# A streaming encoder step on one core: the Silu of c taken once, the cached keys and values split later, a weight split moved behind an eviction

## The chip, the core and the metric

The kernel runs on one core of one Trainium2 chip. Five engines work side by side, each with its own instruction stream: PE (matrix products), ACT (activations and copies), DVE and POOL (elementwise work) and SP (here it only issues DMA transfers). They wait for one another through semaphores. The metric is the device time of one execution in microseconds (us).

## The reference

One trunk layer of a streaming encoder for 1024 prompt tokens and 32 sample tokens, model width 1024, all in float32:

```
mod = silu(c) @ w_ada + b_ada          # six vectors: sh1, sc1, gt1, sh2, sc2, gt2
h   = rmsnorm(x, g_mix) * (1 + sc1) + sh1
u   = h @ w_in                         # attention q, k, v; mLSTM q, k, v, gates; merge gates
ya  = band attention (8 heads x 64, 64-frame chunks, 8 chunks back, relative bias);
      the sample tokens attend to 128 cached keys and values and to themselves
ym  = mLSTM matrix memory (4 heads x 128), head rmsnorm, sigmoid output gate
x   = x + gt1 * ((sigmoid(ga) * (ya @ w_br_att) + sigmoid(gm) * (ym @ w_br_mlstm)) @ w_out)
x   = x + gt2 * ((silu(g) * up) @ w_down),   g, up = split((rmsnorm(x, g_ffn) * (1 + sc2) + sh2) @ w_gate_up)
y   = rmsnorm(x, g_final)
```

There are two vectors c, one for the prompt and one for the sample, of 1024 numbers each. Outputs are y, the new keys and values and the new mLSTM states.

## The kernel before

**Numbers in two parts.** A float32 operand is split into a high part, a copy in the PE's own rounded float32 format, and a low part, the difference. A product is three passes (high by high, low by high, high by low). So each operand costs one copy, mostly on ACT, and one subtraction, on DVE or POOL (`split_to`, L364 and L365; for tokens in head layout `split_heads`, L662 to L665).

**Tokens and blocks.** The 1056 tokens are columns, in three tiles of 352. The input projection runs in blocks of 128 output columns. `unit` (L395) makes one block and one tile: 24 matmuls into one PSUM bank of the pool `mm` (three banks). Each block then has a `put` that evicts the bank.

**Weights.** `Weights.advance` (L67) keeps a queue of blocks: it splits the next blocks while at most two are ahead of the one in use (L364 on ACT, L365 on POOL), and issues the load of a later block on SP (L375), which waits until the raw tile that it overwrites has been split.

**The order of the work is written out by hand** for PE, ACT, DVE and POOL: the order of the program is the order on each engine. Work beside the blocks is placed by `Side`. `unit` calls `side.flush(1)` behind k = 2, 4 and 6, which runs one entry of the list `side.later`, and `side.tick()` behind k = 1, 3, 5 and 7, which advances the generators that run beside the blocks: the attention of a pair of heads (22 steps over a segment) and `ada_rest`.

**The beginning.** `first_units` (L429) computes the first two of the six modulation vectors from `csil`, the Silu of c in column layout (`silu_cols`, L281, from the tile `cols` loaded at L213), on PE (`ada_sums`, L318); `ada_done` (L325) evicts them on ACT (L326, L327). Then come the norm and the first three blocks: keys, values and queries of the first pair of heads. The first two tiles are done for all three blocks at once; the third tile of keys and values is accumulated in the two banks of `psS`. The last line of `first_units`, L565, calls `W.advance()`, which splits the key weights of the second pair of heads. Only then `k_block(0)` (run, L608) evicts the third tile of its keys (`put`, L595 to L606: ACT L601 and L604, DVE L606) and calls `W.advance()` itself (L612). `v_block(0)` (L644) evicts the third tile of its values (L642) and appends four entries to `side.later` (L653): the two halves of the values to be transposed (`v_tail`, L667: PE L674, ACT L662, DVE L665, and with the second half the output copy L631 and its DMA), the sample's values (`v_sample`, L679), and `cache_kv`. `q_block(0)` computes its third tile with `unit`; its `put` is L702, L704, L706 and L686.

**The cached keys and values** are loaded early (L735 to L739). `cache_kv` (L741) splits the keys (ACT L748 twice, DVE L750 twice, each over 64 partitions x 512) and the values (DVE L664 and L665). They are needed by the ninth query tile of each head.

**Attention** (L763). Step i transposes the probabilities of item i - 2 (PE L819 into `psT`, ACT L826, DVE L831), makes the scores of item i (PE L792 into `psS`, DVE L806 adds the bias and takes the maximum, ACT L807 the exponent, DVE L811 and POOL L812 the normalisation) and applies item i - 3 to the values (PE L851 into `psV`, then ACT L857, DVE L858 and L859). `psS`, `psT` and `psV` exist once each.

**The other four modulation vectors** come from `ada_rest` (L1258), on DVE: 128 dot products (L1275) of a weight tile with a broadcast row of Silu(c). For each half of the rows it loads c into all partitions (`crow`, L1266), yields three times, takes the Silu of 128 x 1024 on ACT (L1269), and yields once more. `tmpt` tiles, among them `crow`, share four buffers.

Of the kernel before, what the change touches and what calls it, by code (L numbers as in the profile page):

```python
# [8 lines left out]
F32 = mybir.dt.float32  # L9
F32R = mybir.dt.float32r  # L10
BF16 = mybir.dt.bfloat16
AF = mybir.ActivationFunctionType
# [6 lines left out]
D = 1024  # L19
S = 1024  # L20
TS = 32
# [5 lines left out]
DH = 64  # L27
# [112 lines left out]
def hybrid_stream_step(  # L140
# [10 lines left out]
    pe, act, dve, pool, sp = nc.tensor, nc.scalar, nc.vector, nc.gpsimd, nc.sync  # L151
# [10 lines left out]
    dr = ctx.enter_context(tc.tile_pool(name="scratch", bufs=1, space=DRAM))  # L162
# [16 lines left out]
    def tmpt(shape=(P, T), dt=F32):  # L179
        return tmp.tile(list(shape), dt, tag="t", name=nm("t"))  # L180
# [16 lines left out]
    side = Side()  # L197
    W = Weights()
# [12 lines left out]
    NR = R_C + 16  # L211
    cols = cp.tile([P, NR], F32, name="cols")
    act.dma_start(cols, params)  # L213
    csil = cp.tile([P, KD, 2], F32, name="csil")

    def bc2(ap):
# [64 lines left out]
    def silu_cols():  # L281
        act.activation(csil, cols[:, R_C:R_C + 16].rearrange("p (c k) -> p k c", c=2), AF.Silu)
        dve.scalar_tensor_tensor(gb1, cols[:, R_ADA + 8:R_ADA + 16], 1.0, gm1, op0=ALU.add, op1=ALU.mult)
# [145 lines left out]
    def first_units(put_k, put_v, put_q):  # L429

        early, late = TILES[:2], TILES[2]
        act.activation(silu1, ones, AF.Silu)
        silu_cols()
        for j in range(6):
            pt = mmt()
            ada_sums(j, 0, pt)
            ada_sums(j, 1, pt)
            if j < 3:
                ada_done(j, pt)
            else:  # L440
                n = {3: 2, 4: 6, 5: KD}[j]
                for i in range({3: 0, 4: 2, 5: 6}[j], n):
                    square_sum(i, 0, CUT)
                ada_done(j, pt)
# [117 lines left out]
        for w, n in zip(W.blocks, (3, 3, 2)):  # L562
            for _ in range(n):
                W.used(w)
        W.advance()  # L565

    def units(w):
        done = first.get(id(w))
# [65 lines left out]
    def v_block(hp):  # L634
        w = w_cols(VA + hp * P)

        vfs = []

        def put(lo, hi, pt):
            if lo == 0:  # L640
                vfs.append(tmpt())
            act.activation(vfs[0][:, lo:hi], pt, AF.Copy)  # L642

        def run():  # L644
            for lo, hi, pt in units(w):
                put(lo, hi, pt)
            vf = vfs[0]
            W.advance()
            jobs = [lambda: v_tail(hp, vf, 0), lambda: v_tail(hp, vf, 1), lambda: v_sample(hp, vf)]
            if hp:  # L650
                side.later += [jobs[0], lambda: None, jobs[1], lambda: None, jobs[2]]
            else:
                side.later += jobs + [lambda: cache_kv(early_loads[0])]  # L653
        run.w = w
        run.put = put
        return run

    def split_heads(dst, src, eng=None):

        hi, lo = (dst[:, :, :, 0], dst[:, :, :, 1]) if len(dst.shape) == 5 else (dst[:, :, 0], dst[:, :, 1])  # L660
        if eng is None:
            act.activation(hi, src, AF.Copy)  # L662
        else:
            eng.tensor_copy(hi, src)  # L664
        dve.tensor_tensor(lo, src, f(hi), op=ALU.subtract)  # L665
# [64 lines left out]
    ckv_t = []  # L730
# [7 lines left out]
        sp.dma_start(ckv[:, 1], cache_v[0, 0].rearrange("t h d -> t (h d)"))  # L738
        return ckv  # L739

    def cache_kv(ckv):  # L741
        t = slot([P, 2, 2, 512], F32R)
        cv = t[:, 0].rearrange("p s c -> p (s c)").rearrange("p (h s d) -> p h s d", s=2, d=DH)
        ck = t[:, 1].rearrange("p s (g t) -> p s g t", g=4)
        k4 = ckv[:, 0].rearrange("p (g t) -> p g t", g=4)

        for hh, (u, v) in enumerate(ROWS):
            act.activation(ck[u, hh], k4[u], AF.Copy)  # L748
        for hh, (u, v) in enumerate(ROWS):
            dve.tensor_tensor(ck[v, hh], k4[u], f(ck[u, hh]), op=ALU.subtract)  # L750
        split_heads(cv, ckv[:, 1].rearrange("p (h d) -> p h d", d=DH), dve)
        ckv_t.extend([ck, cv])

    def rel_bias_tile(h):
        bt = ap_.tile([P, WIN], F32, tag="bias", name=nm("bias"))
# [7 lines left out]
    def attention(hp):  # L763
# [69 lines left out]
        def values(it, pv, w):  # L833

            hh, qi = it
            vt, vst, cv = att_v[hp], vst_t[hp], ckv_t[1]
            hd = slice(hh * DH, (hh + 1) * DH)
            if qi % 2 == 0:
                yps[0] = ps_v()
            yp = yps[0]  # L840
            if qi < 8:
                i, c, a = 2, P, (qi - 1) * P
                kb0 = max(0, qi * P - 512) // P
                yo = yp[:, (qi % 2) * 256:(qi % 2 + 1) * 256]
                terms = [(vt[:, kb0 + b, hh], pv[:, :, b * P:(b + 1) * P]) for b in range(w // P)]
            else:
                i, c, a = 1, TS, S
                yo = yp[:, :2 * TS]
                terms = [(cv[:, 2 * hp + hh], pv[:, :, :TS]), (vst[:, hh], pv[:TS, :, TS:2 * TS])]
            for b, (v, p) in enumerate(terms):  # L850
                pe.matmul(yo.rearrange("p (s c) -> p s c", s=2), v.rearrange("p s d -> p (s d)"), p,  # L851
                          start=(b == 0), stop=(b == len(terms) - 1))
            if qi % 2 == 1 or qi == 8:

                q4 = yp[:, :i * 2 * c].rearrange("p (i s c) -> p i s c", i=i, s=2)
                y = yaT[hd, a:a + i * c].rearrange("p (i c) -> p i c", i=i)
                act.activation(y, q4[DH:, :, 0], AF.Copy)  # L857
                dve.tensor_tensor(y, q4[:DH, :, 0], y, op=ALU.add)  # L858
                dve.tensor_tensor(y, q4[:DH, :, 1], y, op=ALU.add)  # L859
# [398 lines left out]
    def ada_rest():  # L1258


        junk = gp.tile([P, 512], BF16, tag="junk", name="junk", bufs=1)
        sums = gp.tile([P, 2, 4, 2, KD], F32, tag="sums", name="sums", bufs=1)
        for half in range(2):
            crow = tmpt((P, 2, 512))
            c0 = c_rows[:, half * 512:(half + 1) * 512]
            sp.dma_start(crow, bass.AP(c0.tensor, c0.offset, [[0, P], [D, 2], [1, 512]]))  # L1266
            for _ in range(3):
                yield
            act.activation(crow, crow, AF.Silu)  # L1269
            yield  # L1270
            for b in range(32):
                wa = ada_tiles.pop(half * 32 + b)
                for c in range(2):
                    at = sums[:, half, b // KD, c, b % KD:b % KD + 1]
                    dve.tensor_tensor_reduce(junk, wa, crow[:, c], 1.0, 0.0, ALU.mult, ALU.add, at)  # L1275
                    if c == 0:
                        ada_load(half * 32 + b + 1)
                    yield
        dve.tensor_tensor(amod2, sums[:, 0], sums[:, 1], op=ALU.add)
        r0 = R_ADA + 2 * KD  # L1280
        bias = cols[:, r0:r0 + 4 * KD].rearrange("p (v j) -> p v j", v=4)
        for c in range(2):
            dve.tensor_tensor(amod2[:, :, c], amod2[:, :, c], bias, op=ALU.add)
        dve.tensor_scalar(s2, s2, 1.0, None, op0=ALU.add)
        dve.tensor_tensor(s2, s2, bc2(cols[:, R_GFFN:R_GFFN + KD]), op=ALU.mult)
# [1048 lines left out]
```

## Time and profile before

| | us |
|---|---|
| runs of the kernel | 1596.14, 1597.57, 1598.13 (median 1597.57) |
| the profiled execution | 1598.06 |
| its span, first to last instruction | 1596.3 |

| engine | busy us | share of the span |
|---|---|---|
| ACT | 796.2 | 50% |
| DVE | 1105.4 | 69% |
| POOL | 421.4 | 26% |

The mean granted PE clock over the span was 0.997. In the views that follow, a row of the timeline has start, duration, engine, line, operation, output and input with partitions x elements, a count, and in brackets the idle time ahead of it with what ended it; instructions of one line are merged. A row of the windows has the stretch, its length, the busy time of PE, PEld (weight load), DVE, ACT and POOL with the number of instructions, the granted clock, the DMA share and the rate.

### The profile page before, as it was taken

The page shows a single profiled execution, that of the slowest core. Times are in us where ns is not written, and L with a number is a line of the kernel's source. Part 1 is how long each engine was busy: PE and PEld are TensorE (multiplying, and loading weights), DVE is VectorE, ACT ScalarE, POOL GpSimd, SP SyncE. Part 2 cuts the span into 40 slices and gives each one's busy share as a digit, 9 for nine tenths or more (in the row PEclk, how much of TensorE's full clock was granted, in tenths as well). Part 3 has the DMA queues.
Part 4 walks back from the last instruction along what each step waited for, and adds up shares of the span by engine and source line. Part 5 has one row for each costly group of instructions (what it writes and reads, how often), then busy time and mean ns, then how long its engine had stood idle before and what let it go on. Part 6 is the DMA issues. An engine that isn't in the chain of part 4 may idle for free.

```text
span 1596.3 us, 27296 instructions
## 1 busy us (share of the span) xinstructions
PE 1568.8 (98%) x10197; PEld 1551.1 (97%) x10197; DVE 1105.4 (69%) x2276; ACT 796.2 (50%) x1748; POOL 421.4 (26%) x439
## 2 busy tenths in 40 slices
PE   8999999999999999999999999999999999999997
PEld 8989999999999999999999999999999999999997
DVE  3756555556776835546654699998898886799755
ACT  3765463544555545444433655554544544545443
POOL 0433242433222311000012100566565650000000
PEclk9999999999999999999999999999999999999999
DMA  9213223243132322675453311213222227427444
GB/s 373 93 59 95 96 83 109 87 132 99 55 95 66 88 85 74 134 256 177 128 149 112 107 55 51 97 55 106 81 80 94 68 77 251 143 80 240 139 135 156
DMA packets 176329, 186.02 MB, mean 117 GB/s; under 512 B 11746, under 2 KB 141446, under 8 KB 176198
## 3 DMA queue, kind: packets, MB, share of 16 engines
q1 hardware_dynamic: 173542, 182.45, 36.5%
q10 hardware_dynamic: 2656, 1.83, 0.4%
q8 instruction: 80, 1.31, 0.4%
q14 instruction: 51, 0.42, 0.1%
HBM read 150.10 MB, written 34.16 MB: 115 GB/s over the span
## 4 chain that ended last, share of the span: by engine, by line
PE 88%; ACT 3%; DVE 3%; DMA 3%; issue 2%; POOL 0%; SPq 0%; ACTq 0%; DVEq 0%; POOLq 0%
PE mm L402 38%; PE psb L1869 18%; PE mm L1869 11%; PE psb L2251 3%; PE mm L946 3%; PE mm L2251 2%; PE psV L851 2%; PE psb L2115 2%; PE psS L792 1%; PE psT L819 1%; PE mm L2115 1%; DMA s<-in_w_ada_dram 1%; DMA s<-in_x_dram 1%; PE psV L1180 1%; PE psT L1182 1%
## 5 line engine op out<-in xcount | busy, mean ns | idle before, releaser
L402 PE MATMUL mm<-s,wsp 128*128 128x352 f32 x4104 | 688.6, 324 | 0.1
L402 PEld LDWEIGHTS mm<-s,wsp 128*128 128x128 f32 x4104 | 658.7, 189 | 2.2 <-issue 0.4
L365 DVE TENSOR_TENSOR wsp<-wraw,wsp 128x512 fp32r<-128x512 f32 (+1 forms) x280 | 236.8, 863 | 118.5 <-ACT wsp L364 115.7
L1869 PE MATMUL psb<-s,wsp 128*128 128x352 f32 x1611 | 271.7, 322 | 1.5 <-DVE wsp L365 0.8
L364 ACT ACTIVATE wsp<-wraw 128x512 fp32r<-128x512 f32 x336 | 200.0, 618 | 139.0 <-PE psb L1869 41.5
L1869 PEld LDWEIGHTS psb<-s,wsp 128*128 128x128 f32 x1611 | 260.6, 188 | 2.1 <-DVE wsp L365 1.1
L1869 PE MATMUL mm<-s,wsp 128*128 128x352 f32 x933 | 159.2, 322 | 0.0
L1869 PEld LDWEIGHTS mm<-s,wsp 128*128 128x128 f32 x933 | 151.2, 188 | 0.5 <-DVE wsp L365 0.3
L812 POOL TENSOR_SCALAR st<-st,mx 128x640 f32<-128x640 f32 (+5 forms) x72 | 53.5, 742 | 188.4 <-DVE mx L811 169.3
L1275 DVE CUSTOM_DVE_ANT_0 junk<-wa,t 128x512 bf16<-128x512 f32 x128 | 94.9, 742 | 1.9 <-DMA wa<-in_w_mod_dram 0.9
L365 POOL TENSOR_TENSOR wsp<-wraw,wsp 128x512 fp32r<-128x512 f32 x56 | 74.1, 1344 | 52.0 <-ACT wsp L364 50.5
L806 DVE CUSTOM_DVE_ANT_0 st<-psS,bias 128x640 f32<-128x640 f32 (+5 forms) x72 | 44.5, 618 | 58.7 <-PE psS L792 44.0
L807 ACT ACTIVATE st<-st,mx 128x640 f32<-128x640 f32 (+5 forms) x72 | 48.1, 668 | 63.4 <-DVE mx L806 62.3
L1816 POOL TENSOR_TENSOR t<-t,sl 128x352 f32<-128x352 f32 x19 | 18.4, 968 | 213.1 <-ACT sl L1814 213.1
L826 ACT ACTIVATE pT<-psT 128x640 fp32r<-128x640 f32 (+3 forms) x80 | 38.6, 494 | 61.6 <-PE psT L819 49.1
L2224 POOL TENSOR_TENSOR fst<-fst,mhalf 128x6 f32<-128x6 f32 x1 | 2.3, 2313 | 221.1 <-DVE fst L2223 221.1
L831 DVE TENSOR_TENSOR pT<-psT,pT 128x640 fp32r<-128x640 f32 (+3 forms) x80 | 44.0, 558 | 23.0 <-ACT pT L826 22.9
L1488 POOL TENSOR_TENSOR wraw<-wraw,raw 128x512 f32<-128x512 f32 x33 | 55.8, 1705 | 0.9
L946 PE MATMUL mm<-s,s 128*128 128x264 f32 (+3 forms) x432 | 54.5, 283 | 0.0
L2251 PE MATMUL psb<-s,wsp 128*128 128x352 f32 x330 | 54.2, 324 | 0.0
L2251 PEld LDWEIGHTS psb<-s,wsp 128*128 128x128 f32 x330 | 53.1, 188 | 0.1
L946 PEld LDWEIGHTS mm<-s,s 128*128 128x128 f32 (+1 forms) x432 | 51.9, 179 | 0.5
(375 smaller groups left out, 2472.5 us busy)
## 6 DMA issues: line engine op xcount, KB each, us to landing
wraw<-in_w_in_dram SPq DMA_DIRECT2D x37, 512.0 KB, 3.6
wraw<-in_w_gate_up_dram SPq DMA_DIRECT2D x33, 512.0 KB, 3.9
wa<-in_w_mod_dram SPq DMA_DIRECT2D x64, 256.0 KB, 2.6
wraw<-in_w_down_dram SPq DMA_DIRECT2D x32, 512.0 KB, 4.3
a_d<-t SPq DMA_DIRECT2D x22, 528.0 KB, 2.7
g_d<-t SPq DMA_DIRECT2D x16, 528.0 KB, 4.2
t<-g_d SPq DMA_DIRECT2D x16, 528.0 KB, 4.8
s<-in_w_ada_dram SPq DMA_DIRECT2D x16, 512.0 KB, 8.8
```

The lines of the kernel that those rows point to most:

```text
L364: act.activation(dst[:, 0], src, AF.Copy)
L365: eng.tensor_tensor(dst[:, 1], src, f(dst[:, 0]), op=ALU.subtract)
L402: pe.matmul(pt[:, :hi - lo], wt[(w0 + k) // 4][:, a, (w0 + k) % 4], xt[k][:, b, lo:hi], start=(k == 0 and q == 0), stop=(k == n - 1 and q ...
L806: dve.tensor_tensor_reduce(so, sv, bi, -1.0, 3.0e38, ALU.add, ALU.min, mx[:n, 1:2])
L807: act.activation(st[:n, :w], st[:n, :w], AF.Exp, bias=mx[:n, 1:2], scale=-1.0, accum_out=mx[:n, 2:3])
L812: pool.tensor_scalar(st[:n, :w], st[:n, :w], mx[:n, 3:4], 1.0, op0=ALU.mult, op1=ALU.mult)
L946: pe.matmul(pt[:n, :wd], hs[k][:, a, i * P:i * P + n], whl[b][:, k, :wd], start=(k == 0 and q == 0), stop=(k == KD - 1 and q == 2))
L1275: dve.tensor_tensor_reduce(junk, wa, crow[:, c], 1.0, 0.0, ALU.mult, ALU.add, at)
L1488: self.eng.tensor_tensor(a(dst), a(x), a(y), op=op)
L1869: pe.matmul(acc, wt[:, a, k], x[k][:, b], start=(start and not onto and k == 0 and q == 0), stop=(stop and k == 3 and q == 2), skip_group_ ...
L2115: pe.matmul(acc, wt[k // 4][:, u, k % 4], piece_of[k, i][:, v], start=(k == 0 and q == 0), stop=(k == KP - 1 and q == 2))
L2251: pe.matmul(acc, wt[(k - k0) // 4][:, u, (k - k0) % 4], piece_of[k, 2][:, v], start=(k == 0 and q == 0), stop=(k == NF - 1 and q == 2))
```

## The change

There are three parts.

1. At the beginning a tile `crows` of 2 partitions x 1024 is loaded with c on ACT's queue, behind the load of `cols`. Behind `silu_cols()` ACT takes its Silu and writes it to a DRAM tile `sil_d`. `ada_rest` loads `crow` from `sil_d` instead of from c, and its own Silu goes; the number of yields stays four.
2. The `W.advance()` at the end of `first_units` goes; the next call is the one in `k_block(0)`, behind the eviction of its third tile.
3. `cache_kv` becomes two functions. The entries of `side.later` are the first half of the values, nothing, the second half, the sample, four times nothing, the cached keys, nothing, the cached values. So the second half of the values and the sample come one entry later, the keys five entries later, and the values two behind these. `values` reads the tile of the cached values only where it is used.

```
+    crows = tmpt((2, D))
+    act.dma_start(crows, c_rows)
+    sil_d = dr.tile([2, D], F32, name="sil_d")
...
         silu_cols()
+        act.activation(crows, crows, AF.Silu)
+        act.dma_start(sil_d, crows)
...
             for _ in range(n):
                 W.used(w)
-        W.advance()
...
-                side.later += jobs + [lambda: cache_kv(early_loads[0])]
+                nothing = lambda: None
+                side.later += [jobs[0], nothing, jobs[1], jobs[2]] + [nothing] * 4
+                side.later += [lambda: cache_keys(early_loads[0]), nothing, lambda: cache_values(early_loads[0])]
...
-    def cache_kv(ckv):
+    def cache_keys(ckv):
         t = slot([P, 2, 2, 512], F32R)
...
+        ckv_t.extend([ck, cv])
...
         for hh, (u, v) in enumerate(ROWS):
             dve.tensor_tensor(ck[v, hh], k4[u], f(ck[u, hh]), op=ALU.subtract)
-        split_heads(cv, ckv[:, 1].rearrange("p (h d) -> p h d", d=DH), dve)
-        ckv_t.extend([ck, cv])
+
+    def cache_values(ckv):
+        split_heads(ckv_t[1], ckv[:, 1].rearrange("p (h d) -> p h d", d=DH), dve)
...
-            vt, vst, cv = att_v[hp], vst_t[hp], ckv_t[1]
+            vt, vst = att_v[hp], vst_t[hp]
...
-                terms = [(cv[:, 2 * hp + hh], pv[:, :, :TS]), (vst[:, hh], pv[:TS, :, TS:2 * TS])]
+                terms = [(ckv_t[1][:, 2 * hp + hh], pv[:, :, :TS]), (vst[:, hh], pv[:TS, :, TS:2 * TS])]
...
-            c0 = c_rows[:, half * 512:(half + 1) * 512]
+            c0 = sil_d[:, half * 512:(half + 1) * 512]
             sp.dma_start(crow, bass.AP(c0.tensor, c0.offset, [[0, P], [D, 2], [1, 512]]))
-            for _ in range(3):
+            for _ in range(4):
                 yield
-            act.activation(crow, crow, AF.Silu)
-            yield
```

## The prediction

> **What bounds the kernel now.** I read the busy shares and the chain on the page, then the list of PE's waits, then the timeline around each wait.
>
> ```profile
> span 1596.3 us, 27296 instructions
> PE 1568.8 (98%) x10197; PEld 1551.1 (97%) x10197; DVE 1105.4 (69%) x2276; ACT 796.2 (50%) x1748; POOL 421.4 (26%) x439
> ...
> PE 88%; ACT 3%; DVE 3%; DMA 3%; issue 2%; POOL 0%; SPq 0%; ACTq 0%; DVEq 0%; POOLq 0%
> ```
>
> PE is busy 98% and holds 88% of the chain. A change elsewhere counts only where it removes or makes idle time on PE, and such a gain moves all that follows forward. Its longest waits behind the start (total us, times, longest):
>
> ```profile
> PE psT L819 <- DVE pT L831: 2.5, 3, 2.0
> PE psV L851 <- ACT pT L826: 2.0, 2, 1.7
> PE mm L674 <- ACT t L642: 1.8, 1, 1.8
> PE psS L792 <- DVE mx L806: 1.4, 1, 1.4
> ```
>
> These hold nearly all that this change can win: 1.8 and 1.4 near 75 and 88 us, 1.7 at 104, 2.0 at 427. The 1.7 has a tail (a row of the windows; the last three numbers are granted clock, DMA share, GB/s):
>
> ```profile
> 104.70:108.10 3.40, 3.40 (x13) 3.40 (x14) 1.95 (x6) 0.92 (x2) 0.80 (x1) 0.50 0.00 0
> ```
>
> For 3.4 us behind that wait PE works at half the clock.
>
> **Part 1: Silu at the beginning.** Added on ACT: the issue of a load of 2 x 1024 floats, one Silu, the issue of a write.
>
> ```profile
> cols<-in_params_dram ACTq DMA_DIRECT2D x1, 62.0 KB, 4.2
> 5.00 0.22 ACT L282 ACTIVATE csil<-cols 128x16 f32<-128x16 f32 x1 [2.25 <-DMA cols<-in_params_dram]
> 10.97 0.36 ACT L326 ACTIVATE s<-mm,gb,cols 128x2 f32<-128x2 f32 x1 [5.75 <-PE mm L321]
> 5.27 23.53 PE L321 MATMUL mm<-csil,s 128*128 128x128 f32 x192 [5.27 <-ACT csil L282]
> 98.25 1.28 ACT L1269 ACT_TABLE_LOAD   x1
> 99.54 1.06 ACT L1269 ACTIVATE t<-t 128x1024 f32<-128x1024 f32 x1
> 101.00 1.28 ACT L807 ACT_TABLE_LOAD   x1
> 65.70 0.38 SPq L1266 DMA_DIRECT2D t<-in_c_rows_dram  x1
> ```
>
> The load's issue falls into ACT's 2.25 us wait for cols. The Silu (1.06, as L1269) and the write's issue (about 0.4) fall into its 5.75 us of idle time; the Silu table is active already. PE waits only for csil, which stands ahead. Taken: 0. Bounds: nothing below, since nothing is removed here; above, the lateness of the new load, see the slower rival. The row of c is read by SP only at 65.70, when its tile comes free, long after the write. The new tile takes one of four, but is free by some 10 us, before the third of the old ones is asked for.
>
> **Part 2: the two Silus of ada_rest go,** each with two table loads: 1.28 + 1.06 + 1.28 = 3.62 us of ACT. The yields stay four, so nothing else in that generator moves. What stood behind the first:
>
> ```profile
> 103.24 0.38 ACT L857 ACTIVATE t<-psV 64x256 f32<-64x256 f32 x1
> 99.38 0.82 DVE L806 CUSTOM_DVE_ANT_0 st<-psS,bias 128x640 f32<-128x640 f32 x1 [0.95 <-POOL st L812]
> 101.72 0.63 PE L819 MATMUL psT<-ident,st 128*128 128x128 f32 x4 [0.31 <-DVE pT L831]
> 104.67 0.96 PE L851 MATMUL psV<-pT,s 128*128 128x256 f32 x3 [1.73 <-ACT pT L826]
> 105.44 4.27 PE L402 MATMUL mm<-s,wsp 128*128 128x352 f32 x18
> 95.27 3.05 PE L402 MATMUL mm<-s,wsp 128*128 128x352 f32 x18
> ```
>
> Without the detour L807 starts when L806 is through (100.2), and L857 at 101.3 instead of 103.24; the two DVE additions behind it (L858, L859) free the bank psV by 102.6, and PE comes at 102.94: both waits go, 0.31 + 1.73. With them goes the halved clock: 18 matmuls in 4.27 instead of 3.05, and the three L851 in 0.96 instead of some 0.5. Sum 2.0 + 1.2 + 0.4 = 3.7. The second, at 415:
>
> ```profile
> 416.93 0.82 DVE L806 CUSTOM_DVE_ANT_0 st<-psS,bias 128x640 f32<-128x640 f32 x1 [0.73 <-PE psS L792]
> 419.43 0.83 ACT L807 ACTIVATE st<-st,mx 128x640 f32<-128x640 f32 x1
> 427.35 0.74 PE L819 MATMUL psT<-ident,st 128*128 128x128 f32 x5 [2.02 <-DVE pT L831]
> ```
>
> L807 can start at 417.8, behind L806, instead of 419.43. From there ACT and DVE run back to back to 427.35, so PE's wait shrinks by 1.6 and 0.4 is left. No halved clock stood behind this one.
>
> **Part 3: key weights split behind the first evictions.** The advance at L565 went ahead of the last third of the keys. It issues two ACT copies, two POOL subtractions and, when these are done, a load on SP.
>
> ```profile
> 72.93 1.16 ACT L364 ACTIVATE wsp<-wraw 128x512 fp32r<-128x512 f32 x2
> 74.11 0.93 ACT L601 ACTIVATE s<-psS 64x352 fp32r<-64x352 f32 x2
> 76.64 0.47 ACT L642 ACTIVATE t<-psS 128x352 f32<-128x352 f32 x1 [1.12 <-DVE s L606]
> 77.16 0.55 PE L674 MATMUL mm<-ident,t 128*128 128x128 f32 x3 [1.78 <-ACT t L642]
> 79.31 6.02 PE L402 MATMUL mm<-s,wsp 128*128 128x352 f32 x36
> 77.70 1.37 DVE L665 TENSOR_TENSOR s<-mm,s 128x512 fp32r<-128x512 f32 x2 [1.09 <-ACT s L662]
> ```
>
> Now the evictions start at 72.95, 1.16 earlier, and the copies (1.16) fill ACT's 1.12 of idle time while DVE subtracts: L642 starts at 75.55, 1.1 earlier. POOL's subtractions start at 75.0 and end by 77.5; POOL's next work is 4 us off, SP's load feeds a block some 20 us off. Besides, the second half of the values is transposed six matmuls (3.05 / 18 x 6 = 1.0) later, at 76.1: the wait of 1.78 is gone. The next block then needs a bank, free when the first L665 ends (1.1 earlier, 77.3): it starts at 77.3, not 79.31. PE is 2.0 ahead.
>
> **Part 4: keys and values of the cache split later.**
>
> ```profile
> 82.56 1.27 ACT L748 ACTIVATE s<-t 64x512 fp32r<-64x512 f32 x2
> 83.27 2.95 DVE L750 TENSOR_TENSOR s<-t,s 64x512 fp32r<-64x512 f32 x2 [1.01 <-POOL s L706]
> 86.25 0.43 DVE L664 CAST s<-t 128x512 fp32r<-128x512 f32 x1
> 86.72 0.69 DVE L665 TENSOR_TENSOR s<-t,s 128x512 fp32r<-128x512 f32 x1
> 87.42 1.06 DVE L606 TENSOR_TENSOR s<-mm,s 64x352 fp32r<-64x352 f32 x2
> 82.69 2.99 POOL L365 TENSOR_TENSOR wsp<-wraw,wsp 128x512 fp32r<-128x512 f32 x2
> 89.45 0.41 DVE L806 CUSTOM_DVE_ANT_0 st<-psS,bias 128x256 f32<-128x256 f32 x1
> 93.42 0.28 DVE L831 TENSOR_TENSOR pT<-psT,pT 128x128 fp32r<-128x128 f32 x1
> 94.47 0.38 PE L819 MATMUL psT<-ident,st 128*128 128x128 f32 x2
> ```
>
> These 4.07 us of DVE stood ahead of L606 and so of the first scores; PE waited 1.4 for their bank. Now L606 runs at 82.5, behind its own eviction, the first L806 at 84.5 (behind POOL's mask), and PE passes without a wait: 3.4 to 3.5 ahead. But the work is moved, not removed. The keys now stand between the first and the second L806, the values between the second and the third. Queued behind them on DVE: L806, L606 of the next third, L831, which frees the one bank pair psT that PE's second L819 needs. With 0.7 for each of the two L750 the chain is: the first exponent ends on ACT at 85.3; L748 runs from there, half of its 1.27 is enough for the first L750 to start at 86.0; the two end at 87.4, the second L806 at 87.9. From the end of the second L806 (89.45 + 0.41 = 89.86) to the end of the first L831 (93.42 + 0.28 = 93.70) it was 3.84 us, a chain of ACT and DVE steps in which PE had no part. It stays, with the values (0.43 + 0.69 = 1.12) added: 87.9 + 3.8 + 1.1 = 92.9, rounded up. PE would be there at 91.2 (94.47 less the 3.4 ahead, rounded up) and waits 1.8; it goes on at 93.0 against 94.47: 1.5 ahead. DVE is only 0.8 ahead then, so the next L831 costs another 0.3: 1.2 ahead.
>
> What one L750 costs in the new place no row shows. Nearest are 0.69 (L665, the same 512 elements from SBUF, POOL idle) and 2.95 / 2 = 1.47 (beside POOL's L365). In the new place POOL has only one scaling of 0.4 us, so I take 0.7 and keep both ends. [...]
>
> **Sum.** Keys, values and weights 1.2, then 3.7 for the first Silu: PE ends the group of 105.44 at 104.8 instead of 109.7, 4.9 ahead. With 1.6 at 427: 6.5. The profiled execution took 1598.06 us, 1.76 beyond its span and 0.5 above the median 1597.57. 1598.06 - 6.5 = 1591.5.
>
> **Rivals.** *A, the keys stay at 1.47 each* (chance 0.20). L831 ends at 94.45, PE gains nothing there and stands still for 3.3 us. Without a halved clock the rest gives 3.4 + 1.6: 1593.1. Halved for 3.4 us as at 104.7, 1.7 lost, 0.3 absorbed: 1594.5. For it: the only two L750 on record. Against: POOL is idle now.
>
> *B, no new wait* (0.10): if DVE's chain is 1.8 shorter than I add up, PE keeps 3.5: 3.5 + 3.7 + 1.6 = 8.8, 1589.3. Against: each link is from a row.
>
> *C, the gain is given back behind 110 us* (0.13): behind 130 us the chain in order of time passes over ACT and DVE several times, and if they, not PE, set the pace there, only the 1.6 of the second Silu survives: 1596.5. Against: the list of PE's waits has none of that stretch among its longest, and what is ahead there is ahead on all engines.
>
> *D, slower* (0.05): ACT works in order and now waits for the row of c ahead of its first L326. PE fills its first bank of three by 10.97 and two more at the mean pace of 16 matmuls (23.53 x 16 / 192 = 2.0 each), to some 15 us; with 1.5 for Silu and issue, each us that the load lands later than 13.5 is lost in full. It decides against the change when 9.3 are lost (1600.8 - 1591.5), a landing after 22.8; at 24 the time is 1602.0. Against: the load ahead on the same queue landed 4.2 us after its issue, beside the same traffic.
>
> *The halved clock after my own 1.8 us wait* belongs to the forecast's range (up to +1.7). The waits of 1.78 and 2.02 quoted above were not followed by it; 0.31 and 1.73 within 3.4 us were. [...]
>
> **How the numbers follow.** Forecast 0.50, A 0.20, B 0.10, C 0.13, D 0.05, 0.02 left over. A measurement tells about 0.2% (3.2 us) from no change: faster is below 1594.4, slower above 1600.8. Faster: forecast, B and most of A, 0.75. Same: C and the rest of A, 0.19. Slower: D, 0.06. The range runs from B's time less 0.3 to A's upper end plus 1: 1589.0 to 1595.5, leaving out C and D.
>
> **What would show it.** Right: no table load between 60 and 110 us beside the first Exp's, clock 1.00 throughout, no wait at L674 nor at the second L792, a new wait of one to two us at the second L819 on L831, L750 near 0.7, PE's wait at 427 (now some 421) near 0.4. Wrong: L750 at 1.4, a window at clock 0.50 near 95, the first L326 waiting for c, or PE's waits growing behind 110.

## The result, and the profile after

The kernel after took 1591.34 us (median of 7 executions, 1591.2 to 1593.19) against 1597.45 (1596.14 to 1598.13, 7 executions) for the kernel before beside it: ratio of the means 0.9966, 95% interval 0.9954 to 0.9977. A second comparison on another chip (experiment 11) gave 1591.18 against 1595.9, 0.9971 (0.9960 to 0.9982). Of the 90 executions of the kernel before in all comparisons one took 2579.6 us at a granted clock of 0.56; it is left out everywhere. The profiled execution took 1591.20 us, 6.86 less than that of before; the prediction had 1591.5.

In the code after, the lines of the prediction stand some lines further down: ACT's copies of the weights L364 are L367, POOL's subtraction L365 is L368, the projection L402 is L405, L642 is L646, the transposes of the values L674 are L680, the keys of the cache L748 and L750 are L755 and L757, the values of the cache L664 and L665 are L670 and L671 (so are those of the sample), the low part of the queries L686 is L692, scores L792 are L800, L806 is L814, the transposes of the exponents L819 are L827, their copy on ACT L826 is L834, their second part L831 is L839, the values L851 are L859. In some of the experiments the same lines stand a few lines up or down; operation and tiles tell which they are.

From the page of after, the span and the engines:

```profile
span 1589.5 us, 27294 instructions
...
PE 1566.5 (99%) x10197; PEld 1549.4 (97%) x10197; DVE 1104.4 (69%) x2276; ACT 788.3 (50%) x1743; POOL 422.1 (27%) x439
```

PE's busy time is 2.3 us less and the span 6.8: most of the gain is idle time of PE that went. Of the 2.3 some 1.6 is work that ran at full instead of half clock: behind the first Silu's place three products with the values and 18 matmuls took 0.96 + 4.27 before and 0.59 + 3.06 after. PE's waits (total us, times, longest):

```profile
PE psT L827 <- DVE pT L839: 2.3, 3, 1.8
...
PE psV L859 <- ACT pT L834: 0.5, 2, 0.3
```

Of the four waits of before, the 1.8 on L642 and the 1.4 at the second scores are off the list, and the 1.7 on the copy of the exponents is down to 0.20 (the row at 101.18; the 0.3 of the list stands at 185 us, as it did before). The wait for pT is still there with 1.8, but at another place: before, its 2.0 stood at 427 us; now its 1.8 stands at 91, ahead of the second L827. The timeline of after shows each step:

```profile
5.11 1.05 ACT L437 ACTIVATE t<-t 2x1024 f32<-2x1024 f32 x1 [0.34 <-DMA t<-in_c_rows_dram]
10.67 0.35 ACT L329 ACTIVATE s<-mm,gb,cols 128x2 f32<-128x2 f32 x1 [4.51 <-PE mm L324]
...
75.28 0.47 ACT L646 ACTIVATE t<-psS 128x352 f32<-128x352 f32 x1
75.94 0.60 PE L680 MATMUL mm<-ident,t 128*128 128x128 f32 x4
77.08 1.73 PE L405 MATMUL mm<-s,wsp 128*128 128x352 f32 x9
...
81.69 1.26 DVE L671 TENSOR_TENSOR vst<-stg,vst 32x128 fp32r<-32x128 f32 x1
84.23 0.29 DVE L814 CUSTOM_DVE_ANT_0 st<-psS,bias 128x128 f32<-128x128 f32 x1 [0.20 <-POOL bias L768]
85.62 1.45 DVE L757 TENSOR_TENSOR s<-t,s 64x512 fp32r<-64x512 f32 x2 [0.36 <-ACT s L755]
88.38 0.27 PE L827 MATMUL psT<-ident,st 128*128 128x128 f32 x1
92.26 0.28 DVE L839 TENSOR_TENSOR pT<-psT,pT 128x128 fp32r<-128x128 f32 x1
92.69 0.41 PE L827 MATMUL psT<-ident,st 128*128 128x128 f32 x2 [1.77 <-DVE pT L839]
96.69 0.52 PE L827 MATMUL psT<-ident,st 128*128 128x128 f32 x3
101.18 0.59 PE L859 MATMUL psV<-pT,s 128*128 128x256 f32 x3 [0.20 <-ACT pT L834]
101.61 3.06 PE L405 MATMUL mm<-s,wsp 128*128 128x352 f32 x18
104.51 0.71 PE L827 MATMUL psT<-ident,st 128*128 128x128 f32 x5
...
420.61 0.73 PE L827 MATMUL psT<-ident,st 128*128 128x128 f32 x5 [0.39 <-DVE pT L839]
```

The Silu lies in ACT's idle time (4.51 us of it are left behind it). The second half of the values is transposed at 75.94 with no wait. The two subtractions of the keys take 1.45 together. The 18 matmuls at 101.61 take 3.06, at full clock. Two rows of before that the prediction does not show, for the first and the third transposes of the exponents:

```profile
92.09 0.27 PE L819 MATMUL psT<-ident,st 128*128 128x128 f32 x1
98.16 0.49 PE L819 MATMUL psT<-ident,st 128*128 128x128 f32 x3
```

How far PE is ahead of before, by the same instruction in both profiles:

| place | before | after | ahead | prediction |
|---|---|---|---|---|
| next block behind the values | 79.31 | 77.08 | 2.2 | 2.0 |
| first transposes of the exponents | 92.09 | 88.38 | 3.7 | 3.4 to 3.5 |
| second transposes of the exponents | 94.47 | 92.69 | 1.8 | 1.5 |
| third transposes of the exponents | 98.16 | 96.69 | 1.5 | 1.2 |
| the transposes behind the first Silu's place | 109.54 | 104.51 | 5.0 | 4.9 |
| the transposes at 427 | 427.35 | 420.61 | 6.7 | 6.5 |

### The profile page after: what moved, and what is told of

It is laid out like the page before. It is cut to its first block, busy times and chain, and to the rows that moved or that the text cites. A ratio compares the mean times of both kernels' runs of the same rounds, so it can differ in the third digit from the quotient of the medians.

```text
span 1589.5 us, 27294 instructions
## 1 busy us (share of the span) xinstructions
PE 1566.5 (99%) x10197; PEld 1549.4 (97%) x10197; DVE 1104.4 (69%) x2276; ACT 788.3 (50%) x1743; POOL 422.1 (27%) x439
## 3 DMA queue, kind: packets, MB, share of 16 engines
q10 hardware_dynamic: 2664, 1.85, 0.4%
## 4 chain that ended last, share of the span: by engine, by line
PE 91%; DVE 3%; ACT 2%; issue 2%; DMA 2%; POOL 1%; ACTq 0%; SPq 0%; DVEq 0%; POOLq 0%
PE mm L405 41%; PE psb L1875 18%; PE mm L1875 11%; PE psb L2257 3%; PE mm L954 3%; PE mm L2257 2%; PE psV L859 2%; PE psb L2121 2%; PE psS L800 2%; PE psT L827 1%; PE mm L2121 1%; DMA s<-in_w_ada_dram 1%; DMA s<-in_x_dram 1%; PE psV L1188 1%; PE psT L1190 1%
## 5 line engine op out<-in xcount | busy, mean ns | idle before, releaser
L405 PE MATMUL mm<-s,wsp 128*128 128x352 f32 x4104 | 687.2, 324 | 0.1
L405 PEld LDWEIGHTS mm<-s,wsp 128*128 128x128 f32 x4104 | 657.3, 188 | 1.9 <-issue 0.4
L368 DVE TENSOR_TENSOR wsp<-wraw,wsp 128x512 fp32r<-128x512 f32 (+1 forms) x280 | 236.4, 861 | 117.3 <-ACT wsp L367 114.1
L367 ACT ACTIVATE wsp<-wraw 128x512 fp32r<-128x512 f32 x336 | 199.5, 617 | 139.9 <-PE psb L1875 43.0
L820 POOL TENSOR_SCALAR st<-st,mx 128x640 f32<-128x640 f32 (+5 forms) x72 | 53.5, 743 | 183.4 <-DVE mx L819 165.4
L368 POOL TENSOR_TENSOR wsp<-wraw,wsp 128x512 fp32r<-128x512 f32 x56 | 74.5, 1351 | 52.5 <-ACT wsp L367 50.2
L814 DVE CUSTOM_DVE_ANT_0 st<-psS,bias 128x640 f32<-128x640 f32 (+5 forms) x72 | 44.5, 618 | 57.4 <-PE psS L800 43.5
L815 ACT ACTIVATE st<-st,mx 128x640 f32<-128x640 f32 (+5 forms) x72 | 47.9, 666 | 64.4 <-DVE mx L814 64.2
L834 ACT ACTIVATE pT<-psT 128x640 fp32r<-128x640 f32 (+3 forms) x80 | 38.6, 493 | 64.2 <-PE psT L827 51.7
L839 DVE TENSOR_TENSOR pT<-psT,pT 128x640 fp32r<-128x640 f32 (+3 forms) x80 | 44.0, 558 | 21.4 <-ACT pT L834 21.3
```

Source lines behind the costliest of these rows:

```text
L367: act.activation(dst[:, 0], src, AF.Copy)
L368: eng.tensor_tensor(dst[:, 1], src, f(dst[:, 0]), op=ALU.subtract)
L405: pe.matmul(pt[:, :hi - lo], wt[(w0 + k) // 4][:, a, (w0 + k) % 4], xt[k][:, b, lo:hi], start=(k == 0 and q == 0), stop=(k == n - 1 and q ...
L814: dve.tensor_tensor_reduce(so, sv, bi, -1.0, 3.0e38, ALU.add, ALU.min, mx[:n, 1:2])
L815: act.activation(st[:n, :w], st[:n, :w], AF.Exp, bias=mx[:n, 1:2], scale=-1.0, accum_out=mx[:n, 2:3])
L820: pool.tensor_scalar(st[:n, :w], st[:n, :w], mx[:n, 3:4], 1.0, op0=ALU.mult, op1=ALU.mult)
```

## The experiments

All were compared with the kernel before on the same chip, in five rounds each. T is the theory of the prediction: DVE's chain gives back part of what the moved split wins, and the two Silus hold the greatest share.

**1. The Silu part alone, in the kernel before.** The kernel before with the lines of the first part of the diff (crows, sil_d, the load from sil_d, four yields without Silu); the rest unchanged.

> The kernel before with only the Silu of c moved to the beginning; the weight split and the cached keys and values stay where they were. Theory T (a wait counts only as far as the next wait on DVE does not take it back): waits of 1.8 at the transposes and 1.4 at the second scores stay, those of 0.3 and 1.7 near 102 to 105 us and the halved clock go (3.7), the wait at 427 falls from 2.0 to 0.4 (1.6): 5.3 faster than before, some 1592.2. Rival R (the three parts each carry about a third to a half): 3 faster, some 1594.4.

Measured: 1592.43 us (1592.11 to 1592.59, 10 executions) against 1596.1, ratio 0.9978 (0.9969 to 0.9987). The time is the one that T gave, the difference is not: 3.7 less than the kernel before on this chip, where T had 5.3 and R had 3. T's waits alone are 3.7; the other 1.6 of its 5.3 is the halved clock, which T took from one profile of the kernel before. So the time does not decide between T and R, but the waits do. PE's waits in its profile:

```profile
PE mm L679 <- ACT t L647: 1.7, 1, 1.7
PE psS L797 <- DVE mx L811: 1.4, 1, 1.4
```

The two waits that the other parts were to remove are there in full; those behind the Silus are not. And 3.7 is more of the whole change's 4.7 to 6.1 than R's third to half.

**2. The change without its Silu part.** The kernel after with these lines of before again:

```
+            c0 = c_rows[:, half * 512:(half + 1) * 512]
-            c0 = sil_d[:, half * 512:(half + 1) * 512]
...
+            act.activation(crow, crow, AF.Silu)
```

> The changed kernel with the Silu of c put back into the generator; the weight split and the cached keys and values stay late. T: the waits at the transposes and at the second scores are gone, the new wait of 1.8 at the second transposes of probabilities stands, and near 104 us PE meets the two table loads again with ACT only 1.0 ahead of before; the clock is halved behind that wait: 1.0 faster than before, some 1596.5. R: 3 faster, 1594.4.

Measured: 1596.3 us (1594.76 to 1596.48, 11 executions), ratio 0.9998 (0.9989 to 1.0007): the other two parts without the Silu do not show beside the kernel before. The time is T's again, R's 1594.4 fell; of T's difference of 1.0 the medians show nothing. The path is not the one that T thought of: the wait behind the first Silu stood at 1.74 us and the clock behind it was full. The half clock came at 425 instead. The timeline there, and the windows:

```profile
424.38 0.95 PE L822 MATMUL psT<-ident,st 128*128 128x128 f32 x5 [2.00 <-DVE pT L834]
424.98 1.41 PE L795 MATMUL psS<-s,s 128*128 128x320 f32 x4
```

```profile
421.36:424.77 3.41, 1.41 (x11) 1.14 (x10) 3.03 (x9) 1.11 (x3) 0.00 (x0) 1.00 0.00 0
424.77:428.18 3.41, 3.41 (x17) 3.06 (x15) 2.17 (x6) 2.62 (x7) 3.24 (x3) 0.50 0.24 79
```

Four L795 take 1.41 instead of some 0.84. So the halved clock is not tied to one place; the last section comes back to it. A fair partner for this profile is that of experiment 8, in which the kernel before has its one halved window at 425 too: 1597.19 there against 1596.27 here, 0.9 less, near T's 1.0 (two single executions, on two chips).

**3. The cached keys and values early, as before.** The kernel after with

```
-                side.later += [jobs[0], nothing, jobs[1], jobs[2]] + [nothing] * 4
-                side.later += [lambda: cache_keys(early_loads[0]), nothing, lambda: cache_values(early_loads[0])]
+                side.later += [jobs[0], nothing, jobs[1]]
+                side.later += [lambda: (cache_keys(early_loads[0]), cache_values(early_loads[0])), jobs[2]]
```

> The changed kernel with the cached keys and values split where they were before, at the first entry of the next block. T: the second scores wait again, 2.4 us now because PE comes earlier, but the wait at the second transposes of probabilities goes; the two cancel within 0.5: 1591.2 to 1591.9, or 1.7 more if 2.4 us at a stretch halve the clock. R: moving the cache late is worth its old wait, so 1.4 lost: 1592.7.

Measured: 1593.72 us (1592.21 to 1594.1), ratio 0.9982 (0.9973 to 0.9991): 4 of 11 executions at 1592.2 to 1592.9, 7 at 1593.6 to 1594.1. T's two numbers were 1591.2 to 1591.9, and 1.7 more where the clock is halved. R's 1592.7 lies as near to the lower group as T's, so the time does not decide; T's exchange of waits is there (no wait of PE on L839 above 0.4 is left), its price is 0.5 off. The timeline of the profiled execution (1593.57) shows why:

```profile
81.33 3.00 POOL L368 TENSOR_TENSOR wsp<-wraw,wsp 128x512 fp32r<-128x512 f32 x2
81.90 2.97 DVE L757 TENSOR_TENSOR s<-t,s 64x512 fp32r<-64x512 f32 x2 [1.00 <-POOL s L712]
86.53 0.28 DVE L671 TENSOR_TENSOR vst<-stg,vst 32x128 fp32r<-32x128 f32 x1
88.26 0.71 PE L800 MATMUL psS<-s,s 128*128 128x256 f32 x2 [3.08 <-DVE mx L814]
```

PE waits 3.1 us at the second scores where T had 2.4: here the sample's values (0.8 us of DVE) stand behind the cache and ahead of the first L814, which T had left out. The first two rows also settle what one subtraction of the keys costs: 2.97 for two beside POOL's L368, as before, and 1.45 for the same two in the kernel after, where POOL has only a scaling of 0.38 beside the first of them. So the shape alone is not slow: what differs between the two rows is the neighbour. The sample's subtraction shows the same: 0.28 here with POOL idle, 1.26 in the kernel after, where it runs beside POOL's L368 (81.53 to 84.11). A subtraction with one operand in PSUM took the same beside an L368 and without one: in the kernel after (s<-mm,s) 0.69 at 76.34, beside the L368 that ends at 77.35, and 0.69 at 77.20, all but 0.15 of it behind that end. Taken one by one, the two L750 of the first profile of before end 0.55 us behind the L365 that ran beside each (84.53 behind 83.98, 86.22 behind 85.67); without that neighbour one takes 0.69 to 0.73 (the two L757 of the kernel after). An estimate from these numbers is that most of each was done only when POOL's instruction was through; what held it until then was not shown.

**4. The advance where it was.** The kernel after with `W.advance()` at the end of `first_units` again.

> The changed kernel with the advance at the end of first_units put back ahead of the evictions. T: the copies again hold the evictions back by 1.1 us; a wait of some 0.6 at the transposes, and the whole chain on ACT and DVE to the second transposes of probabilities is 1.1 later: 1592.4. R: the old wait of 1.8 comes back: 1593.1. If only the later place of the transposes counted: no difference, 1591.3.

Measured: 1592.35 us (1591.96 to 1594.01), ratio 0.9975 (0.9967 to 0.9984); T had 1592.4, the rivals 1593.1 and 1591.3. Two of the 11 executions took 1593.8 and 1594.0; the profile is of the longest. PE's waits in it:

```profile
PE psT L828 <- DVE pT L840: 2.2, 3, 1.6
...
PE mm L681 <- ACT t L647: 0.7, 1, 0.7
```

The wait on the eviction comes back with 0.7 of its 1.8 (the rest is hidden by the values' later place), and the next block starts behind DVE (0.25 at L405), so about 1.1 us is what the advance's new place is worth (1592.35 against the 1591.2 to 1591.3 of the kernel after on two other chips).

**5. The keys' subtraction issued twice.** The kernel after with

```
             dve.tensor_tensor(ck[v, hh], k4[u], f(ck[u, hh]), op=ALU.subtract)
+            dve.tensor_tensor(ck[v, hh], k4[u], f(ck[u, hh]), op=ALU.subtract)
```

> The kernel after, with the two DVE subtractions of the cached keys each issued twice (the same result, 1.45 us more on DVE between the first and the second L814). Theory T (the chain of ACT and DVE from the first exponent to the first L839 sets when the second L827 can go, and PE's wait of 1.8 us there is its end): the wait grows by 1.4 to some 3.2 us, all behind it is 1.4 later: 1592.7 us, or 1.5 more (1594.2) in executions in which the clock is halved behind that wait, as it was behind the wait of 3.1 in the experiment with the cache early. Rival R (the wait has slack, something else ends it): 1591.3 us, wait 1.8.

Measured: 1593.56 us, ratio 0.9984 (0.9975 to 0.9993): 3 of 11 executions at 1592.4 to 1592.7, 8 at 1593.5 to 1594.1. T's two groups are both there, the upper some 0.5 below its 1594.2; no profile fell on that one. The profile is of one of the lower (1592.74):

```profile
88.75 0.61 PE L801 MATMUL psS<-s,s 128*128 128x384 f32 x2 [0.37 <-DVE mx L815]
93.86 0.41 PE L828 MATMUL psT<-ident,st 128*128 128x128 f32 x2 [2.58 <-DVE pT L840]
```

1.4 us more on DVE made PE 1.17 later at the second transposes (93.86 against 92.69): 0.37 of it at the scores ahead of them, the rest in the wait, 2.58 against 1.77 (T had 3.2). On DVE itself all of it arrives: from the first L815 to the first L840 it is 9.47 us (83.96 to 93.43), and 8.03 in the kernel after (84.23 to 92.26), 1.44 more. The profile of 5 was 0.27 ahead before the chain began, which is the difference to 1.17. DVE's chain does end that wait.

**6 and 7. Both, or only the values, later still.** In 6 the cached keys and values are split four entries later, in the next block; in 7 only the values, two entries later:

```
+                side.later += [jobs[0], nothing, jobs[1], jobs[2]] + [nothing] * 8
+                side.later += [lambda: cache_keys(early_loads[0]), lambda: cache_values(early_loads[0])]
...
+                side.later += [lambda: cache_keys(early_loads[0])] + [nothing] * 3
+                side.later += [lambda: cache_values(early_loads[0])]
```

> The kernel after, with the cached keys and values split four entries later still, inside the next block of the first unit of attention (behind the third transposes instead of between the scores). Theory T: the first L839 ends 1.45 + 1.1 = 2.5 us earlier, so the wait of 1.8 us at the second L827 is gone, and the 0.2 to 0.3 behind it; a part may come back at a later transpose (at most 0.5 us, as DVE is idle more often there): 1589.3 to 1589.8 us, 1.5 to 2.0 below the kernel after. Rival R (the split costs the same PE time wherever it stands, as DVE has no idle time before the first values): the wait only moves, 1591.3 us.

> The kernel after, with the cached keys where they are and only the cached values split two entries later, inside the next block. Theory T: DVE's chain to the first L839 is 1.1 us shorter, the wait at the second L827 falls from 1.8 to 0.7 us: 1590.2 us, about half of what moving both gives. Rival R (the wait only moves): 1591.3 us.

Measured: 6 took 1591.09 us (1590.9 to 1592.52, ratio 0.9968, 0.9957 to 0.9979), 7 took 1590.95 (1590.49 to 1592.49, the same ratio and interval). T fell here: it had 1589.3 to 1589.8 and 1590.2. The timeline of 6, and then that of 7:

```profile
94.89 1.84 DVE L757 TENSOR_TENSOR s<-t,s 64x512 fp32r<-64x512 f32 x2 [0.35 <-ACT s L755]
99.27 0.63 PE L827 MATMUL psT<-ident,st 128*128 128x128 f32 x4 [1.71 <-DVE pT L839]
101.50 4.59 PE L405 MATMUL mm<-s,wsp 128*128 128x352 f32 x18
```

```profile
91.72 0.41 PE L828 MATMUL psT<-ident,st 128*128 128x128 f32 x2 [0.63 <-DVE pT L840]
96.87 1.06 DVE L672 TENSOR_TENSOR s<-t,s 128x512 fp32r<-128x512 f32 x1
101.08 0.59 PE L860 MATMUL psV<-pT,s 128*128 128x256 f32 x3 [0.57 <-ACT pT L835]
101.51 3.06 PE L405 MATMUL mm<-s,wsp 128*128 128x352 f32 x18
```

In 6 the second transposes go without a wait, at 90.63, and the fourth wait 1.71 in their place. In 7 the wait is cut into 0.63, 0.30 and 0.57. Either way the 18 matmuls start at 101.50 or 101.51, against 101.61 in the kernel after. (The profile of 6 is its longest execution; the 4.59 is again a halved window, 101.46 to 104.88 at clock 0.50.) Judged by the time the rival was right: at these places, from 85 to 101 us, the work on DVE cost PE nearly the same (1591.34 us in the kernel after, 1591.09 and 1590.95 here). One reason may be that the chain over DVE and ACT has little slack there; another is POOL. In 7 the copy and the subtraction of the values took 0.64 + 1.06 beside POOL's L368 and L821 (0.43 + 0.69 in the kernel after), in 6 the two keys 1.84 beside POOL's L820 (1.45). If all of these 0.6 and 0.4 us reached PE, they would be most of what T missed in 7 and a smaller part of it in 6; no run takes the two reasons apart.

**8. The kernel before once more**, unchanged, for a second profile.

> The kernel before, unchanged, for a second profile of it: its times fell into groups some 1.5 us apart. Theory T (what sets the groups apart is whether PE's clock is halved for one window of some 3.4 us behind one of its waits): its waits are those of the first profile within 0.2 us, and a profiled execution that takes 1.5 us less or more than 1598.1 shows one window at clock 0.50 fewer or more, or the window at another place. Rival R (the groups come from DMA or from the start): the same single window near 105 us, and waits that differ.

Measured: 1597.19 us (1594.14 to 1597.6), ratio 1.0004 (0.9995 to 1.0013). The profiled execution took 1597.19. Its waits are those of the first profile (2.0, 1.7, 1.7, 1.4). The windows behind the two Silus:

```profile
101.44:104.85 3.41, 1.68 (x12) 1.45 (x13) 1.70 (x6) 2.72 (x6) 0.80 (x1) 1.00 0.02 7
...
422.29:425.70 3.41, 1.41 (x11) 1.14 (x10) 3.02 (x9) 1.11 (x3) 0.00 (x0) 1.00 0.00 0
425.70:429.11 3.41, 3.41 (x17) 3.06 (x15) 2.17 (x6) 2.65 (x7) 3.24 (x3) 0.50 0.33 79
```

The same kernel, the same waits, and the clock is halved at 425.7 and not at 104.7. From the wait at 104 to the next transposes it took 3.32 us here (104.29 to 107.61) and 4.87 in the first profile (104.67 to 109.54); from 427 on it is the other way round, 7.32 (425.30 to 432.62) against 5.86 (427.35 to 433.21). One halved window costs 1.5 us, at either place.

**9 and 10. The split in front of the chain.** If no place between 80 and 101 us is free, one ahead of it may be: DVE stood idle for 1.97 us ahead of L692 in the kernel after. In 9 keys and values go there, in 10 the keys alone:

```
+                side.later += [jobs[0], nothing]
+                side.later += [lambda: (jobs[1](), cache_keys(early_loads[0]), cache_values(early_loads[0])), jobs[2]]
...
+                side.later += [jobs[0], nothing, lambda: (jobs[1](), cache_keys(early_loads[0])), jobs[2]]
+                side.later += [nothing] * 6 + [lambda: cache_values(early_loads[0])]
```

> The kernel after, with the cached keys and values split two entries earlier than the sample's values, right behind the second half of the values of the tokens, where DVE stood idle for 1.97 us (77.9 to 79.86) and POOL's subtraction of the key weights had ended (77.35). Theory U (between 80 and 101 us DVE has no idle time that PE could use, so the split's 2.6 us cost the same wherever they stand in it, and only work put into DVE's idle time ahead of it is free): two L757 of 0.7 each at 77.9 to 79.4, the values to 80.5, what follows on DVE 0.6 later and the first scores with it, but the wait of 1.8 at the second L827 falls to about 0.3: 1589.5 to 1590.0 us. Rival V (the idle time is taken by something not seen, or ACT, which has to make the copies first, is late): a wait at the first or second L800 takes its place, 1591.3 us or more.

> The kernel after, with only the cached keys split at that earlier place and the values where they are now. Theory U: the keys' 1.45 us fit into the idle 1.97 us, nothing behind them is late, DVE's chain to the first L839 is 1.45 shorter: the wait of 1.8 falls to about 0.4 and the time to 1589.8 us. Rival V: 1591.3 us.

Measured: 9 took 1591.46 us (1591.28 to 1593.44, ratio 0.9972, 0.9962 to 0.9982): no gain, as rival V had it. 10 took 1590.39 (1590.29 to 1590.72, ratio 0.9965, 0.9952 to 0.9977), 0.8 less than the kernel after on the same chip (experiment 11: 1590.97 to 1592.74, so the two do not overlap) and the least of all; U had 1589.8 and V 1591.3, and it lies between. From the timeline of 10:

```profile
79.22 1.29 ACT L755 ACTIVATE s<-t 64x512 fp32r<-64x512 f32 x2 [0.50 <-ACT stg L635]
79.94 1.40 DVE L757 TENSOR_TENSOR s<-t,s 64x512 fp32r<-64x512 f32 x2 [1.85 <-ACT s L755]
...
92.26 0.41 PE L827 MATMUL psT<-ident,st 128*128 128x128 f32 x2 [0.40 <-DVE pT L839]
```

from that of 11:

```profile
92.85 0.41 PE L827 MATMUL psT<-ident,st 128*128 128x128 f32 x2 [1.79 <-DVE pT L839]
```

and from that of 9:

```profile
82.44 2.33 DVE L692 TENSOR_TENSOR s<-t,s 64x352 fp32r<-64x352 f32 x2
...
87.76 0.51 PE L800 MATMUL psS<-s,s 128*128 128x256 f32 x2 [1.70 <-DVE mx L814]
```

The idle time was not used: DVE's 1.97 us is still there as 1.85, since DVE now waits for ACT's copies, and these delay the evictions behind them. L692 is 1.4 later than in 11 (81.38 against 80.01). The wait of 1.79 falls to 0.40, but PE arrives 0.8 later, and 0.59 remains at the second transposes (92.26 against 92.85); the two profiled executions are 0.61 apart (1590.72 and 1591.33). In 9 the first L814 is so late that the second scores wait 1.70 us, the place that V had named; there the two L692 also take 2.33 beside POOL's L712 and L368, against 1.24 in the kernel after, where L368 started only behind them (81.53). Theory U had looked at DVE's idle time and not at the engine that feeds it; V had.

**11. The kernel after once more**, as the measure for 9 and 10.

> The kernel after, unchanged, as the measure for the other two on the same chip: 1591.2 to 1591.8 us, or 1.5 more in the executions with a halved window. Its profile shows the same waits as the first one (1.8 at the second L827) within 0.2 us; if it falls into the higher group, one window at clock 0.50.

Measured: 1591.18 us (1590.97 to 1592.74, 7 executions, six of them up to 1591.33). The profile shows 1.79 at the second L827 and 0.38 at 421.

## Why the prediction was right

*Part 1, the Silu at the beginning, 0.* Right: the row of c landed early enough for ACT to start at 5.11 us, no table load stood at it (the first two of the kernel after are at 1.80 and 82.47), and 4.51 us of idle time were left behind it. The slower rival, a late landing, did not come up.

*Part 2, 3.7 for the first Silu and 1.6 for the second.* The waits behaved as worked out (104: 0.2 left; 427: 0.39 left against 0.4). The 1.6 of the halved clock was right for the profiled execution, but read as a fixed part of the kernel before, which it is not: experiment 8 has it at the other Silu, and the times fall into groups some 1.5 us apart, which suggests, though no profile shows it, that some executions have none. So one profile cannot give the size of this term. The comparison on the other chip, where before had a median of 1595.9, shows 4.7 in place of 6.1, and the sum without the 1.6 is 4.9. That the difference of the first comparison came so near to 6.5 was in part luck: the seven executions of before beside it happened to have a median of 1597.45.

*Part 3, 2.0 for the key weights.* Right: 2.2 measured at the next block, 0.13 of which was there at 31 us (31.31 against 31.18), behind a beginning that the loads set.

*Part 4, 3.4 won and 2.2 given back.* Right in mechanism and size: the first L814 at 84.23 (84.5), the L757 at 0.72 each (0.7, chosen between 0.69 and 1.47 as POOL had little to do there), the wait of 1.77 (1.8), the second transposes at 92.69 (93.0). PE was 3.7 ahead at the first transposes and 1.5 at the third, 2.2 given back. Both ends of the wait came 0.3 earlier than worked out, at 90.92 (91.2) and 92.69 (93.0), so its length fits better than either. What the prediction did not see is why so little stays: it is no accident of the five entries. Experiments 6 and 7 moved the same work on and lost nearly all of it again.

*The rivals.* A, the keys at 1.47 each, fell: 0.72. Experiment 3 is what the trace of before could not show: the same instruction takes 1.49 beside POOL's L368 and 0.72 in the new place. B, no new wait, fell with the 1.77. C, the gain given back behind 110 us, fell with the 6.7 at 427. The half clock behind the new wait of 1.8, which the prediction kept in its range and left out of its sum as an estimate, did not come in the two profiles of the kernel after (one execution in seven of each comparison, 1593.19 and 1592.74, lies 1.6 to 1.9 above the median and was not profiled); why it is close is told below.

The parts do not simply add, as far as runs on different chips can tell: beside the kernel before the Silu alone took 3.7 us off and the other two parts nothing in the median, and yet they take 1.1 us more off the Silu kernel's 1592.4.

## What to carry to other kernels

Before moving work off one wait, look at the chain of engines behind its new place, and behind the place ahead: here, at three places between 85 and 101 us, the work cost nearly the same (1591.34 us in the kernel after, 1591.09 and 1590.95 in experiments 6 and 7). A place in front of the whole chain helped here only for the smaller piece, by 0.6 to 0.8 us, because the idle time there was a wait for ACT: ask what ends an idle stretch before filling it. Look at the neighbour too: a DVE subtraction of two operands in SBUF took twice its time and more beside a subtraction on POOL (1.49 against 0.72, 1.26 against 0.28). Price a wait of PE by what it does to the clock too: here stretches of 3.41 us with some 2 us of idle time (1.37 and 1.41 busy) were followed by a half clock that cost 1.5 more. So take a term such as a halved window from several executions, not from one profile.

## What the runs showed of the hardware

**In these profiles the clock was halved on a fixed raster of 3.41 us.** Read in windows of 0.1 us, the clock falls to 0.50 at the end of each profile too, behind the last matmul, where it costs nothing. From the start of the halved window inside the same profile to that fall it is in each a whole number of times the same length. One halved window lasted 3.41 us, and the differences between the distances fix the length to 3.4133 (1553.06 - 1163.94 = 389.12, 114 lengths):

| profile | halved from | falls at the end | distance | whole number x 3.4133 |
|---|---|---|---|---|
| before, first | 104.69 | 1589.49 | 1484.80 | 435 |
| before, second (8) | 425.71 | 1589.65 | 1163.94 | 341 |
| without the Silu part (2) | 424.77 | 1588.72 | 1163.95 | 341 |
| cache early (3) | 88.38 | 1586.83 | 1498.45 | 439 |
| advance kept (4) | 32.10 | 1585.16 | 1553.06 | 455 |
| cache in the next block (6) | 101.46 | 1582.85 | 1481.39 | 434 |

Each lasted 3.41 us. At 8.2 to 11.1 us the pace of PE's first matmuls rises in all thirteen profiles at a mark of the same raster, 460 to 463 lengths ahead of the fall: the first profile of before has 18 matmuls from 5.70 to 9.12 and 32 from 9.12 to 12.53 (the clock column reads 1.00 in both, so that this rise is one of the clock is an estimate from the pace). The fall comes 1.1 to 4.0 us behind the last matmul, and the rise not at one time, so in these profiles the raster does not start with the kernel. In each of them the fall at the end tells where the raster lies, and each wait can be laid on it. Windows cut on the raster, from the first profile of before (the second column of numbers is PE's busy time):

```profile
101.28:104.69 3.41, 1.37 (x10) 1.03 (x9) 1.46 (x5) 3.26 (x6) 0.80 (x1) 1.00 0.10 40
104.69:108.11 3.42, 3.42 (x13) 3.42 (x14) 1.96 (x6) 0.92 (x2) 0.80 (x1) 0.50 0.00 0
...
425.54:428.96 3.42, 1.61 (x13) 1.63 (x13) 2.55 (x9) 2.32 (x7) 1.03 (x1) 1.00 0.00 0
```

The same from experiment 3, around its wait of 3.08 us:

```profile
84.96:88.38 3.42, 0.34 (x3) 0.12 (x2) 3.09 (x9) 0.14 (x1) 0.00 (x0) 1.00 0.51 158
88.38:91.79 3.41, 3.41 (x13) 3.41 (x14) 1.13 (x5) 2.20 (x7) 0.85 (x2) 0.50 0.00 0
```

from experiment 5, around its wait of 2.58:

```profile
88.85:92.26 3.41, 2.43 (x14) 2.15 (x14) 1.67 (x5) 1.90 (x6) 0.48 (x1) 1.00 0.00 0
92.26:95.68 3.42, 1.82 (x12) 1.77 (x13) 1.69 (x6) 2.11 (x6) 0.59 (x1) 1.00 0.00 0
```

and from the kernel after, around its wait of 1.77:

```profile
90.58:94.00 3.42, 1.65 (x12) 1.30 (x10) 2.05 (x6) 1.60 (x5) 0.60 (x1) 1.00 0.00 0
```

Between 25 us and the end, the thirteen profiles have four raster windows in which PE is busy for 1.41 us or less, and each is followed by one at half clock; of eleven with 1.59 to 1.71, one is (1.61, in experiment 6). The wait of 2.58 in experiment 5 lay across a mark, 2.43 and 1.82 busy, and was not followed by a halved window; the 2.0 of before was followed by one where a mark lay 0.4 us behind its end (425.30 and 425.70 in experiment 8, 424.38 and 424.77 in 2), and not in the first profile, where the mark lay 1.6 us behind (427.35 and 428.96). So the same wait cost 1.5 us in one execution and nothing in another. It fits that the Silu kernel of experiment 1, whose longest waits behind the start are 1.7 and 1.4, kept within 0.5 us in ten executions, and that the 1.77 of the kernel after, wholly inside one window with 1.65 busy, is a close miss beside the 1.61 of experiment 6. The window ahead of a halved one need not be idle throughout: in the first profile of before PE was busy for 40% of it (1.37 of 3.41 us).

Three things stay open. In experiment 4 the window behind the one from 28.69 to 32.10, in which PE was busy for 2.27 us, was halved; the matmuls there are those of the first stage, of another shape, and whether that is the reason was not shown. Why one window with 1.61 busy was followed by a halved one and another with 1.59 was not, the busy times do not tell. And 13 of the 89 other executions of the kernel before took 1594.1 to 1594.7, some 1.5 us less than the 1595.7 that the profiled 1597.19 less one halved window would give; no profile fell on one of them. So the halved windows inside the kernel explain a distance of 1.5 us between executions, but not all of the groups.
